# Seven half-size block products for the SwiGLU behind the convolution, and another spread of the adaLN chunks

## The chip, the cores and the metric

The kernel runs on one core of one Trainium2 chip, in one launch. The metric is the device time of an execution in microseconds (us). Of the kernel before there are three timed runs and one profiled execution. Engines are called as the profile calls them: PE (matrix products), PEld (its weight loads), DVE (VectorE), ACT (ScalarE), POOL (GpSimd), SP (SyncE, which issues nearly all transfers).

## The reference, cut to what matters

Two layers work on 256 latent tokens x and 256 context tokens z, 1024 features each. A layer is a SwiGLU, a token mixer (a short convolution in the first layer, attention in the second) and another SwiGLU, each between norms that shift, scale and gate by vectors made from a condition c (adaLN):

```python
mx = (silu(c) @ w_mod[i] + b_mod[i]).reshape(B, 9, 1, D)      # shift, scale, gate for three sublayers
mz = (silu(c_ctx) @ w_mod[i] + b_mod[i]).reshape(9, D)

def ffn_sublayer(x, mod, k, g_pre, g_post, w_gu, w_down):
    h = rmsnorm(x, g_pre) * (1 + mod[k + 1]) + mod[k]
    gu = h @ w_gu                                              # 1024 -> 2 * 2816
    y = (silu(gu[..., :2816]) * gu[..., 2816:]) @ w_down       # 2816 -> 1024
    return x + 0.5 * mod[k + 2] * rmsnorm(y, g_post)
```

All values are float32. The output is the latent stream.

## The kernel before

**Products.** Features lie on the 128 partitions, tokens along the free axis (512 columns: 256 of x, 256 of z). A float32 operand is split into a high part that the PE reads at full rate and the rest (`hi`, `lo`), and one product is three: hi·hi, lo·hi, hi·lo (lines 441 to 443, in `groups`). Weights come as slots: 512 KB, eight blocks of 128 by 128, loaded by SP, then split: ACT writes `whi` (line 252), DVE or POOL subtracts to get `wlo` (line 253). The set `POOL` names the slots whose subtraction POOL does. Eight split slots are held in a ring.

**Stages.** Stage 0 is the first SwiGLU, then comes the convolution, stage 2 is the SwiGLU behind it, stage 3 the first SwiGLU of the second layer; then attention and a last SwiGLU on x alone. The 22 gate/up tiles (128 hidden features each) of a SwiGLU are cut into three chunks (`CHUNKS`): gate/up of a chunk, then its share of the down projection in eight jobs of one output tile each. In the first chunk a job's result is copied into `y` by ACT, in the second DVE adds it (line 589), and the third goes through the tail, where the norms of x and z run beside products. Products go to four PSUM banks in turn (`ps`, four buffers): one bank per job of the down projection, two per gate/up tile.

**Head.** The first tiles of a stage are done for x alone while the norm of z still runs, then for z alone: 256-column products.

**Pairs.** In stage 3 alone (`SEVEN = {3: 4}`), tiles 4 to 21 go in nine pairs through `pair` (line 525 is its product): two tiles by 1024 features, times the two token halves, as a 2 by 2 block product in seven products of half size in place of eight (Strassen's way in Winograd's form). One product of the seven is 24 products of the PE at 256 columns. `forms` makes the four sums of the activations once, on DVE and ACT. A pair loads four raw slots; DVE adds weights (line 289, `summed`) and splits the sums (line 278), POOL subtracts for three raw slots (line 281, not by the set `POOL`), and DVE and ACT combine the results (lines 552 to 569). From the first stage with pairs on, raw slots alternate between two rings of three (`two_rings`).

**adaLN chunks.** The vectors come in 18 modules (`MODS`) of eight chunks. `mod_step` fetches the next 512 KB chunk (`wmd`, two buffers) and takes the product sum of the one before on DVE (`dot`, line 340): two sums per chunk in modules 0 to 13 (x and z), one in 14 to 17. `pacer` spreads the steps of a stage evenly over its jobs: `NMODS` says up to which module a stage goes. The jobs are the gate/up tiles outside head and pairs, and the 16 jobs of the first two down projections; `mods_until` does what is left before the tail. With `(7, 6, 15)` stage 0 takes 56 steps (its first 16 chunks come ahead), the convolution none, stage 2 takes 48 and stage 3 the last 24.

**Order.** PE's order is the order of the program text. On the other engines a scheduler orders the instructions; the product sums, the adds into `y` and the products with the gate (line 481) stay in program order among themselves.

Of the kernel before, what the change touches and what calls it, by code (L numbers as in the profile page):

```python
# [27 lines left out]
KT = D // P  # L28
# [1 line left out]
N = 2 * S  # L30
DFF = 2816
FT = DFF // P
CHUNKS = {0: ((0, 7), (7, 14), (14, 22)), 2: ((0, 7), (7, 14), (14, 22)), 3: ((0, 6), (6, 14), (14, 22))}

SEVEN = {3: 4}
HQ, HKV, HD = 16, 4, 64
GRID_W = 64
EPS = 1e-6
# [11 lines left out]
CONV_HEAD = 2  # L50
AT_TAIL = [(2.34, 3.97, 15.14, 16.36), (2.26, 3.97, 15.49, 17.43), (2.59, 3.6, 14.42, 17.25), (2.03, 2.96, 12.85, 16.35)]
AT_HEAD = [(2.1, 4.38, 12.64, 12.75), (3.64, 4.86, 13.86, 15.27), (3.45, 5.01, 14.82, 16.43), (1.54, 2.67, 12.39, 14.05)]
NMODS = (7, 6, 15)
PACE = 1
QUERIES = [(0, 1), (2, 3), (4,), (5,)]
LATE = 16
# [3 lines left out]
ATT = "s0 q6 s0 q7 x0 p s1 p s1 t00 x1 s2 r0 t01 t02 r1 s2 t03 v00 s3 v01 t10 t11 v02 s3 t12 v03 t13 v10 v11 t20 v12 s4 t21 v20 s4 v13 t22 t23 s5 t30 v21 s5 t31 v22 v30 v23 t32 t33 s6 t40 v31 s6 t41 v40 v32 o000 o001 t42 v41 v33 t43 o002 s7 t50 t51 o003 v50 v42 v43 s7 t52 t60 o010 v51 t53 t61 v52 v60 o011 t62 v53 t70 v61 t71 v62 t72 v70 t63 o012 v71 v63 t73 o013 v72 v73 o100 o101 o102 o103"  # L60
EXPT = 1
SCALE = "VAAG"
POOL = {0, 256, 2, 3, 1, 259, 260, 263, 264, 147, 148, 155, 156, 163, 165, 169, 170, 54, 56, 58, 60, 61, 64, 68, 71, 72, 78, 91, 92, 94, 95, 223, 97, 99, 230, 103, 104, 233, 106, 235, 108, 236, 240, 114, 243, 245, 246, 247, 248, 249, 255}

X = slice(0, S)
Z = slice(S, N)
# [15 lines left out]
def tiles_of(w):  # L82

    k, m = w.shape
    return w.reshape(k // P, P, m // P, P).transpose(2, 0, 1, 3)
# [14 lines left out]
def ffn_slots(w_gu, w_down, chunks, seven=FT):  # L100
    gu = tiles_of(w_gu)
    dn = tiles_of(w_down)
    out = []
    for a, b in chunks:
        c = min(max(a, seven), b)
        if a < c:
            out.append(slots_of(np.stack([gu[a:c], gu[FT + a:FT + c]], 1).reshape(-1, P, P)))
        for m in range(c, b, 2):

            for f, k in ((FT, 0), (0, 0), (0, 4), (FT, 4)):  # L110
                out.append(slots_of(gu[f + m:f + m + 2, k:k + 4].reshape(-1, P, P)))
        out.append(slots_of(dn[:, a:b].reshape(-1, P, P)))
    return out


def lay_out(i):
    f = np.float32
    w = []
    w += ffn_slots(i["ffn_w_gu"][0, 0], i["ffn_w_down"][0, 0], CHUNKS[0])

    w[0][:4] = slots_of(w[0][:4].reshape(4, P, KT, P).transpose(2, 0, 1, 3).reshape(-1, P, P))
    ci = tiles_of(i["conv_w_in"][0]).reshape(3, 8, KT, P, P)
    w.append(slots_of(ci[[1, 2, 0]].transpose(1, 0, 2, 3, 4).reshape(-1, P, P)))
    w.append(slots_of(tiles_of(i["conv_w_out"][0]).reshape(-1, P, P)))
    w += ffn_slots(i["ffn_w_gu"][0, 1], i["ffn_w_down"][0, 1], CHUNKS[2])
    w += ffn_slots(i["ffn_w_gu"][1, 0], i["ffn_w_down"][1, 0], CHUNKS[3], SEVEN[3])
    qkv = i["attn_w_qkv"][0]
    pm = q_perm()
    q = slots_of(tiles_of(qkv[:, pm]).reshape(-1, P, P))
    v = qkv[:, D + 256:].reshape(2, 4, P, 256).transpose(0, 2, 1, 3).reshape(2, P, 1024)  # L130
    w += [q[:6], slots_of(tiles_of(qkv[:, D:D + 256]).reshape(-1, P, P)), v, q[6:]]
    w.append(halves_of(i["attn_w_o"][0][pm]))

    gu = tiles_of(i["ffn_w_gu"][1, 1]).reshape(2, FT, KT, P, P)
    w.append(slots_of(gu.transpose(1, 0, 2, 3, 4).reshape(-1, P, P)))
    w.append(halves_of(i["ffn_w_down"][1, 1]))
    wst = np.concatenate(w, 0)

    wm = i["w_mod"].reshape(2, D, 9, D).transpose(0, 2, 3, 1)
    wm = np.stack([wm[l, c] for l, c, _ in MODS]).reshape(len(MODS), KT, P, D)  # L140


    front = wm[:2].copy()
    wm[0] = front[:, DOTS].transpose(1, 0, 2, 3).reshape(KT, P, D)
    wide = front[:, PAIRS].reshape(2, 2, 2, P, KT, P).transpose(1, 4, 5, 0, 2, 3).reshape(2, 4, 2, P, 512)
    wm[1] = wide.transpose(0, 1, 3, 2, 4).reshape(KT, P, D)
    bm = i["b_mod"].reshape(2, 9, KT, P)
    bm = np.stack([bm[l, c] for l, c, _ in MODS]).transpose(2, 0, 1)
    ng = i["norm_g"].reshape(12, KT, P).transpose(2, 0, 1)
    cw = i["conv_w"][0].reshape(3, KT, P).transpose(2, 0, 1)  # L150
    xz = np.concatenate([i["x"][0], i["ctx"][0]], 0).reshape(N, KT, P).transpose(2, 1, 0)


    d = np.arange(HD)
    axis, half, quar = d // 32, (d // 16) % 2, d % 16
    tok = np.arange(S)
    inv = f(10000.0) ** (-(np.arange(16, dtype=f)) / f(16))
    pos = np.stack([(tok // GRID_W).astype(f), (tok % GRID_W).astype(f)])
    ang = pos[axis] * inv[quar][:, None]
    cos = np.tile(np.cos(ang), (2, 1)).astype(f)  # L160
    sin = np.tile(np.sin(ang), (2, 1)).astype(f)
    rot = np.zeros((P, P), f)
    for o in range(P):
        if half[o % HD] == 0:
            rot[o + 16, o] = -1.0
        else:
            rot[o - 16, o] = 1.0
    a = np.arange(P)
    m0 = np.where(a[None, :] <= a[:, None], 0.0, -1e30).astype(f)
    m1 = np.where(a[:, None] <= a[None, :], 0.0, -1e30).astype(f)  # L170
    cst = np.concatenate([cos, sin, cos * f(HD ** -0.5), sin * f(HD ** -0.5), rot, m0, m1], 1)
    cc = np.stack([i["c"].reshape(D), i["c_ctx"].reshape(D)])
    cp = cc.reshape(2, KT, P).transpose(2, 1, 0)
    vec = np.concatenate([cp.reshape(P, -1), bm.reshape(P, -1), ng.reshape(P, -1), cw.reshape(P, -1)], 1)
    arrays = dict(xz=xz, wst=wst, wmd=wm.reshape(-1, P, D), vec=vec, cst=cst, cc=cc.reshape(1, 2 * D),
                  snk=i["attn_sink"].reshape(1, HQ))
    return {k: np.ascontiguousarray(a) for k, a in arrays.items()}
# [6 lines left out]
class Kernel:  # L184
# [427 lines left out]
        return self.norms(1, y, parts[1], nxt)  # L612

    def pacer(self, nmods, njobs):
        todo = nmods * KT - self.mod_at
        state = [0, 0]

        def pace(weight=1):
            state[0] += weight
            while state[1] < min(todo, -(-todo * state[0] // njobs)):  # L620
                self.mod_step()
                state[1] += 1
        return pace

    def ffn(self, l, j, nxt, nmods, pending):
# [4 lines left out]
        m0 = sum(map(len, HEADS[3 * l + j - 1][0])) if pending else 2  # L630
        pace = self.pacer(nmods, PACE * (SEVEN.get(3 * l + j, FT) - m0) + 16)
        if 3 * l + j == min(SEVEN):
            self.two_rings = base
        forms = None
        for ci, (a, b) in enumerate(CHUNKS[3 * l + j]):
            nk = b - a
# [9 lines left out]
            else:  # L646
                for _ in self.gate_up(ALL, base, range(m0), act):
                    next(start, None)
            seven = SEVEN.get(3 * l + j, FT) - a
            for m in range(m0, min(nk, seven)):  # L650
                self.weave([self.gate_up(ALL, base, [m], act)])
                pace(PACE)
            if 3 * l + j in SEVEN and forms is None:
                forms = self.forms()
# [586 lines left out]
```

## Time and profile before

| | us |
|---|---|
| median of three runs | 1683.94 |
| lowest, highest | 1678.51, 1684.57 |
| profiled execution | 1679.4 |
| its span | 1677.6 |
| PE busy | 1631.8 (97%) |
| DVE busy | 1142.7 (68%) |
| ACT busy | 695.4 (41%) |
| POOL busy | 321.6 (19%) |

The profiled execution is a fourth run of its own; its span is what its instructions cover. On PE the page counts products as overlapping, so one product is shown longer than it takes in a row; the time of a stretch divided by the products in it tells what one costs.

### The profile page before, as it was taken

The numbers are of one execution on the slowest core, as the hardware profiler recorded it, in microseconds if no ns is written. First come the engines' busy times: TensorE is split into PE (matmuls) and PEld (weight loads), VectorE is DVE, ScalarE is ACT, GpSimd is POOL, SyncE is SP. The second block draws the span as 40 slices with busy tenths as digits, with TensorE's granted clock in tenths as the row PEclk, the third lists the DMA queues.
The fourth block names the chain that finished last, engine by engine and source line by source line (L and its number), as shares of the span: only waits on it lengthen the run. The fifth ranks groups of instructions, "written<-read, shape, count | busy, mean of one in ns | idle before, by whom it ended". The sixth has DMA issues, their size and how long they took to land.

```text
span 1677.6 us, 25175 instructions
## 1 busy us (share of the span) xinstructions
PE 1631.8 (97%) x10026; PEld 1439.4 (86%) x10026; DVE 1142.7 (68%) x1747; ACT 695.4 (41%) x1166; POOL 321.6 (19%) x214
## 2 busy tenths in 40 slices
PE   8899999999999999999999998999999989989998
PEld 3688888889988998888888998899899887889987
DVE  7769779866744365876965489387785678665553
ACT  4522221325423643322222444354255558654442
POOL 1100000125102431000110421231232664130000
PEclk9999999999999999999999999999999999999999
DMA  9556556653232215664664215334634221045550
GB/s 354 170 169 225 191 186 215 200 175 102 88 101 89 76 52 175 214 193 157 213 199 158 84 50 191 124 101 155 210 103 137 93 88 64 26 164 193 193 181 25
DMA packets 70313, 246.83 MB, mean 147 GB/s; under 512 B 7730, under 2 KB 10290, under 8 KB 70196
## 3 DMA queue, kind: packets, MB, share of 16 engines
q1 hardware_dynamic: 69908, 245.02, 43.8%
q8 instruction: 78, 1.28, 0.3%
q14 instruction: 39, 0.32, 0.1%
q10 hardware_dynamic: 288, 0.20, 0.0%
HBM read 244.15 MB, written 1.05 MB: 146 GB/s over the span
## 4 chain that ended last, share of the span: by engine, by line
PE 88%; DVE 6%; ACT 2%; issue 1%; POOL 1%; DMA 1%; SPq 0%; DVEq 0%; POOLq 0%; ACTq 0%
PE mm L443 23%; PE mm L442 23%; PE mm L441 23%; PE mm L525 10%; DVE junk L340 1%; PE po L947 1%; PE mm L1071 1%; PE mm L1072 1%; PE mm L1070 1%; PE tp L933 1%; POOL acc L402 1%; PE mm L893 1%; DMA xr<-in_xz 1%; DVE wlo L253 1%; PE prb L361 0%
## 5 line engine op out<-in xcount | busy, mean ns | idle before, releaser
L441 PE MATMUL mm<-hh,whi 128*128 128x512 f32 (+1 forms) x1232 | 436.8, 355 | 6.2 <-ACT hh L451 5.0
L252 ACT ACTIVATE whi<-raw 128x1024 fp32r<-128x1024 f32 x280 | 292.3, 1056 | 355.7 <-PE mm L443 291.5
L443 PE MATMUL mm<-hl,whi 128*128 128x512 f32 (+1 forms) x1232 | 435.0, 353 | 1.6 <-DVE hl L416 1.5
L442 PE MATMUL mm<-hh,wlo 128*128 128x512 f32 (+1 forms) x1232 | 435.1, 353 | 0.0
L253 DVE TENSOR_TENSOR wlo<-raw,whi 128x1024 fp32r<-128x1024 f32 x229 | 290.7, 1279 | 113.8 <-ACT whi L252 112.5
L340 DVE CUSTOM_DVE_ANT_0 junk<-wmd,sc,vec 128x1024 bf16<-128x1024 f32 x232 | 307.9, 1327 | 20.4 <-DMA wmd<-in_wmd 16.7
L443 PE MATMUL mm<-al,whi 128*128 128x256 f32 (+1 forms) x848 | 275.9, 325 | 3.3 <-DVE al L569 3.3
L441 PE MATMUL mm<-ah,whi 128*128 128x256 f32 (+1 forms) x848 | 277.0, 327 | 1.7 <-ACT ah L568 1.7
L442 PE MATMUL mm<-ah,wlo 128*128 128x256 f32 (+1 forms) x848 | 275.8, 325 | 0.0
L253 POOL TENSOR_TENSOR wlo<-raw,whi 128x1024 fp32r<-128x1024 f32 x51 | 128.2, 2518 | 753.6 <-ACT whi L252 750.0
L441 PEld LDWEIGHTS mm<-hh,whi 128*128 128x128 f32 x1232 | 233.4, 189 | 42.4 <-ACT hh L451 6.3
L443 PEld LDWEIGHTS mm<-hl,whi 128*128 128x128 f32 x1232 | 233.5, 190 | 34.1 <-DVE hl L416 2.1
L442 PEld LDWEIGHTS mm<-hh,wlo 128*128 128x128 f32 x1232 | 233.7, 190 | 32.7
L443 PEld LDWEIGHTS mm<-al,whi 128*128 128x128 f32 x848 | 161.0, 190 | 18.4 <-DVE al L569 4.8
L441 PEld LDWEIGHTS mm<-ah,whi 128*128 128x128 f32 x848 | 161.1, 190 | 16.5 <-ACT ah L568 2.1
L442 PEld LDWEIGHTS mm<-ah,wlo 128*128 128x128 f32 x848 | 161.1, 190 | 13.6
L479 ACT ACTIVATE sg<-mm 128x512 f32<-128x512 f32 (+1 forms) x78 | 38.6, 495 | 227.4 <-PE mm L443 227.3
L481 DVE TENSOR_TENSOR pr<-mm,sg 128x512 f32<-128x512 f32 (+1 forms) x78 | 43.7, 560 | 128.7 <-PE mm L443 81.5
L281 POOL TENSOR_TENSOR wlo<-raw,whi 128x1024 fp32r<-128x1024 f32 x27 | 68.3, 2530 | 215.7 <-ACT whi L280 199.8
L443 PE MATMUL mm<-h,whi 128*128 128x256 f32 x352 | 99.0, 281 | 0.0
L441 PE MATMUL mm<-h,whi 128*128 128x256 f32 x352 | 98.9, 281 | 0.0
L442 PE MATMUL mm<-h,wlo 128*128 128x256 f32 x352 | 98.7, 280 | 0.0
(226 smaller groups left out, 2480.0 us busy)
## 6 DMA issues: line engine op xcount, KB each, us to landing
raw<-in_wst SPq DMA_DIRECT2D x316, 512.0 KB, 3.6
wmd<-in_wmd SPq DMA_DIRECT2D x140, 512.0 KB, 4.1
xr<-in_xz SPq DMA_DIRECT2D x2, 1024.0 KB, 9.9
wmq<-in_wmd SPq DMA_DIRECT2D x8, 256.0 KB, 7.8
out_y<-xt SPq DMA_DIRECT2D x3, 256.0 KB, 2.1
rtab<-in_cst SPq DMA_DIRECT2D x1, 512.0 KB
out_y<-xt SPq DMA_DIRECT2D x2, 128.0 KB, 1.9
msk<-in_cst ACTq DMA_DIRECT2D x1, 192.0 KB, 4.1
```

What stands on the lines that cost most here:

```text
L252: nc.scalar.activation(hi, raw, AF.Copy)
L253: d = sub.tensor_tensor(lo, raw, hi.bitcast(F32), ALU.subtract)
L281: self.nc.gpsimd.tensor_tensor(lo, src, hi.bitcast(F32), ALU.subtract)
L340: self.keep(self.nc.vector.tensor_tensor_reduce(junk, wt, self.sc[v], 1.0, b, ALU.mult, ALU.add, out))
L402: nc.gpsimd.tensor_tensor(acc, acc, sq, ALU.add)
L441: nc.tensor.matmul(pt[:, :n], whi, rhi[:, sl], start=i == 0, stop=False)
L442: nc.tensor.matmul(pt[:, :n], wlo, rhi[:, sl], start=False, stop=False)
L443: nc.tensor.matmul(pt[:, :n], whi, rlo[:, sl], start=False, stop=i == last)
L479: nc.scalar.activation(sg[:, :n], pg[:, :n], AF.Silu)
L481: self.keep(nc.vector.tensor_mul(pr[:, :n], pu[:, :n], sg[:, :n]))
L525: mm = lambda w, r, start=False, stop=False: nc.tensor.matmul(out, w, r, start=start, stop=stop, skip_group_check=True)
L893: nc.tensor.matmul(sp[e], act[4 * p2 + 2 * jp + jj][x][rows[e], qs], kt[p2][w][rows[e], :], start=a == 0, stop=False)
```

## The change

Stage 2 gets what stage 3 has: `SEVEN` names it too, its chunks become 6, 8 and 8 tiles, and its weights are laid out for `pair`. The raw slots take two rings from stage 2 on. `NMODS` becomes `(8, 11.25, 13.5)`: with module counts in fractions (hence the `int`), stage 0 takes 64 steps, the convolution 10, stage 2 takes 18 and stage 3 takes 36. In stage 3 four of these have two sums each, the other 32 one: 40 sums where there were 24. In stage 2 the 18 steps have 36 sums where there were 88. From the set `POOL` six slots of stage 2 go: 106, 108, 147, 148 and 155 are raw slots of pairs now, 114 is one of the first down projection.

```diff
-CHUNKS = {0: ((0, 7), (7, 14), (14, 22)), 2: ((0, 7), (7, 14), (14, 22)), 3: ((0, 6), (6, 14), (14, 22))}
-
-SEVEN = {3: 4}
+CHUNKS = {0: ((0, 7), (7, 14), (14, 22)), 2: ((0, 6), (6, 14), (14, 22)), 3: ((0, 6), (6, 14), (14, 22))}
+
+SEVEN = {2: 4, 3: 4}
...
-NMODS = (7, 6, 15)
+NMODS = (8, 11.25, 13.5)
...
@@ lay_out
-    w += ffn_slots(i["ffn_w_gu"][0, 1], i["ffn_w_down"][0, 1], CHUNKS[2])
+    w += ffn_slots(i["ffn_w_gu"][0, 1], i["ffn_w_down"][0, 1], CHUNKS[2], SEVEN[2])
...
@@ pacer
-        todo = nmods * KT - self.mod_at
+        todo = int(nmods * KT) - self.mod_at
```

DVE in stage 2, where the first chunk's gate/up ends and its down projection begins. Before, `pr` and `al` finish tile 6 there, between a subtraction for a coming slot and two sums of an adaLN chunk (`junk`, two per chunk):

```order
L481 TENSOR_TENSOR pr<-mm,sg 128x512
L253 TENSOR_TENSOR wlo<-raw,whi 128x1024
L452 TENSOR_TENSOR al_5043<-pr,ah_5042 128x512
L340 ISA junk,mod_1_0_5686<-wmd,sc_95,vec 128x1024
L340 ISA mod_1_0_5686 128x1
L340 ISA junk,mod_1_1_5687<-wmd,sc_96,vec 128x1024
```

Now the first chunk's only pair ends there, and these rows run from the combining of its products to the first two of its four `al` (line 569):

```order
L563 TENSOR_TENSOR mm<-gz,mm 128x512
L560 TENSOR_TENSOR mm<-mm,gx 128x512
L340 ISA junk,mod_2_1_4521<-wmd,sc_96,vec 128x1024
L340 ISA mod_2_1_4521 128x1
L253 TENSOR_TENSOR wlo<-raw,whi 128x1024
L289 TENSOR_TENSOR sum<-raw 128x512 x2
L569 TENSOR_TENSOR al_5155<-mm,ah_5154 128x256 x2
L340 ISA junk,mod_2_0_4520<-wmd,sc_95,vec 128x1024
L340 ISA mod_2_0_4520 128x1
L569 TENSOR_TENSOR al_5157<-mm,ah_5156 128x256 x2
```

The four `al`, which the down projection reads, stand behind the combining, the sums of weights (`sum`) and, counted from the stage's head on, nine sums of adaLN chunks. In stage 3 eight such sums stood ahead of the last `al`, now nine.

DVE in stage 0, second down projection, from the first add into `y` to the second:

```order
L589 TENSOR_TENSOR y<-y,mm 128x512
L340 ISA junk,mod_5_0_1501<-wmd,sc_95,vec 128x1024
L340 ISA mod_5_0_1501 128x1
L340 ISA junk,mod_5_1_1502<-wmd,sc_96,vec 128x1024
L340 ISA mod_5_1_1502 128x1
L334 SCALAR_TENSOR_TENSOR mod_5_0_1501<-mod_5_0_1501,vec 128x8
L589 TENSOR_TENSOR y<-y,mm 128x512
```

The same stretch of the changed kernel:

```order
L589 TENSOR_TENSOR y<-y,mm 128x512
L340 ISA junk,mod_7_0_1689<-wmd,sc_95,vec 128x1024
L340 ISA mod_7_0_1689 128x1
L340 ISA junk,mod_7_1_1690<-wmd,sc_96,vec 128x1024
L340 ISA mod_7_1_1690 128x1
L253 TENSOR_TENSOR wlo<-raw,whi 128x1024
L340 ISA junk,mod_7_0_1689<-wmd,sc_95,vec 128x1024
L340 ISA mod_7_0_1689 128x1
L340 ISA junk,mod_7_1_1690<-wmd,sc_96,vec 128x1024
L340 ISA mod_7_1_1690 128x1
L589 TENSOR_TENSOR y<-y,mm 128x512
```

Between these two adds stand four sums in place of two, and a subtraction. Over the eight adds, from the first to the last, 20 sums and 7 subtractions became 24 and 8.

DVE in stage 3, second down projection, at the same place:

```order
L589 TENSOR_TENSOR y<-y,mm 128x512
L340 ISA junk,mod_6_0_9309<-wmd,sc_95,vec 128x1024
L340 ISA mod_6_0_9309 128x1
L253 TENSOR_TENSOR wlo<-raw,whi 128x1024
L340 ISA junk,mod_6_0_9309<-wmd,sc_95,vec 128x1024
L340 ISA mod_6_0_9309 128x1
L589 TENSOR_TENSOR y<-y,mm 128x512
```

The same stretch of the changed kernel:

```order
L589 TENSOR_TENSOR y<-y,mm 128x512
L340 ISA junk,mod_7_0_10326<-wmd,sc_95,vec 128x1024
L340 ISA mod_7_0_10326 128x1
L253 TENSOR_TENSOR wlo<-raw,whi 128x1024
L340 ISA junk,mod_7_0_10326<-wmd,sc_95,vec 128x1024
L340 ISA mod_7_0_10326 128x1
L340 ISA junk,mod_7_0_10326<-wmd,sc_95,vec 128x1024
L340 ISA mod_7_0_10326 128x1
L589 TENSOR_TENSOR y<-y,mm 128x512
```

Here three sums, each of another chunk, stand where two stood; over the whole down projection and just behind it 18 chunks in place of 12.

## Rows read from the trace of the kernel before

**Rows 1.** The page: span, busy time by engine, and shares of the last chain.
```profile
span 1677.6 us, 25175 instructions
PE 1631.8 (97%) x10026; PEld 1439.4 (86%) x10026; DVE 1142.7 (68%) x1747; ACT 695.4 (41%) x1166; POOL 321.6 (19%) x214
...
PE 88%; DVE 6%; ACT 2%; issue 1%; POOL 1%; DMA 1%; SPq 0%; DVEq 0%; POOLq 0%; ACTq 0%
```

**Rows 2.** Stretches: the length behind the window, then busy time by engine.
```profile
core 0: us, PE busy (x) PEld busy (x) DVE busy (x) ACT busy (x) POOL busy (x), PEclk, DMA share, GB/s
447.90:546.80 98.90, 98.90 (x435) 81.16 (x434) 45.05 (x52) 30.77 (x39) 12.14 (x5) 1.00 0.32 107
611.50:914.50 303.00, 303.00 (x1443) 253.71 (x1442) 214.52 (x298) 89.76 (x120) 18.40 (x7) 1.00 0.55 178
...
826.60:914.50 87.90, 87.90 (x386) 72.13 (x385) 56.47 (x72) 24.72 (x31) 11.17 (x4) 1.00 0.58 187
985.40:1281.50 296.10, 288.62 (x2078) 272.03 (x2077) 223.79 (x342) 139.73 (x230) 70.72 (x28) 0.98 0.42 141
985.40:1017.40 32.00, 29.51 (x231) 28.69 (x230) 30.64 (x53) 14.32 (x29) 2.49 (x1) 0.95 0.06 21
...
1037.30:1077.70 40.40, 35.42 (x146) 27.84 (x145) 19.15 (x32) 12.11 (x20) 4.83 (x2) 0.92 0.49 165
1157.50:1201.70 44.20, 44.20 (x194) 36.03 (x194) 33.34 (x49) 9.80 (x14) 6.23 (x2) 1.00 0.60 203
1201.70:1281.50 79.80, 79.80 (x673) 79.78 (x672) 64.14 (x96) 47.22 (x77) 27.24 (x11) 1.00 0.44 146
238.60:277.00 38.40, 38.40 (x169) 31.51 (x168) 36.37 (x54) 7.95 (x8) 0.00 (x0) 1.00 0.68 219
```

**Rows 3.** Waits of PE in stage 3's head for z: total, times, longest.
```profile
PE mm L443 <- DVE hl L416: 1.5, 2, 1.0
PE mm L441 <- ACT hh L415: 1.0, 1, 1.0
```

**Rows 4.** Timeline of PE behind stage 3's first pair: start, duration, instruction, [idle <-releaser].
```profile
1042.31 0.40 PE L442 MATMUL mm<-ah,wlo 128*128 128x512 f32 x1
1045.76 0.79 PE L443 MATMUL mm<-al,whi 128*128 128x512 f32 x1 [3.05 <-DVE al L569]
...
1047.63 0.79 PE L443 MATMUL mm<-al,whi 128*128 128x512 f32 x1 [0.22 <-DVE al L569]
1048.22 0.63 PE L441 MATMUL mm<-ah,whi 128*128 128x512 f32 x1
```

**Rows 5.** DVE from 1017.4 to 1047.6 by groups: count, busy, mean ns, idle before.
```profile
L340 DVE CUSTOM_DVE_ANT_0 junk<-wmd,sc,vec 128x1024 bf16<-128x1024 f32 x8 | 11.7, 1467 | 0.6 <-DMA wmd<-in_wmd 0.6
L253 DVE TENSOR_TENSOR wlo<-raw,whi 128x1024 fp32r<-128x1024 f32 x5 | 6.1, 1218 | 0.1
```

**Rows 6.** Timelines of DVE and of POOL from 1022 to 1026.
```profile
1023.12 2.81 DVE L340 CUSTOM_DVE_ANT_0 junk<-wmd,sc,vec 128x1024 bf16<-128x1024 f32 x1
...
1022.09 2.76 POOL L281 TENSOR_TENSOR wlo<-raw,whi 128x1024 fp32r<-128x1024 f32 x1 [0.98 <-ACT whi L280]
```

**Rows 7.** Lines 340 and 310 from 985 to 1210: ns or us min/median/max.
```profile
L340 DVE CUSTOM_DVE_ANT_0 junk<-wmd,sc,vec x24: 1270/1280/3301, 1021.3 to 1205.3; 128x1024 bf16<-128x1024 f32 x24
...
  DMA wmd<-in_wmd: 7.0, 6
...
DMA to landing us min/median/max: 3.4/4.4/5.9
```

**Rows 8.** Timeline of DVE in stage 3's second down projection.
```profile
1164.78 0.68 DVE L589 TENSOR_TENSOR y<-y,mm 128x512 f32<-128x512 f32 x1
1165.38 1.28 DVE L340 CUSTOM_DVE_ANT_0 junk<-wmd,sc,vec 128x1024 bf16<-128x1024 f32 x1
1166.59 0.08 DVE L340 DVE_READ_ACCUMULATOR2_ANT mod<- 128x1 f32 x1
```

**Rows 9.** Line 589 from 240 to 296: ns, first and last start.
```profile
L589 DVE TENSOR_TENSOR y<-y,mm x8: 680/684/685, 247.8 to 289.2; 128x512 f32<-128x512 f32 x8
```

**Rows 10.** Line 281: POOL's subtractions in the pairs.
```profile
L281 POOL TENSOR_TENSOR wlo<-raw,whi x27: 2402/2416/3269, 1008.3 to 1265.7; 128x1024 fp32r<-128x1024 f32 x27
```

More of the change, by code (lines that the diff above doesn't have):

```diff
@@ L62 @@
 SCALE = "VAAG"
-POOL = {0, 256, 2, 3, 1, 259, 260, 263, 264, 147, 148, 155, 156, 163, 165, 169, 170, 54, 56, 58, 60, 61, 64, 68, 71, 72, 78, 91, 92, 94, 95, 223, 97, 99, 230, 103, 104, 233, 106, 235, 108, 236, 240, 114, 243, 245, 246, 247, 248, 249, 255}
+POOL = {0, 256, 2, 3, 1, 259, 260, 263, 264, 156, 163, 165, 169, 170, 54, 56, 58, 60, 61, 64, 68, 71, 72, 78, 91, 92, 94, 95, 223, 97, 99, 230, 103, 104, 233, 235, 236, 240, 243, 245, 246, 247, 248, 249, 255}
 X = slice(0, S)
```

## Prediction

> **What bounds the kernel now.** I read the page's busy shares first. PE is busy for 1631.8 of 1677.6 us, and it holds 88% of the chain that ended last; DVE has 6%, all others together 6% [rows 1]. So the time is the number of products by their spacing, plus the few places where PE starves. Next I cut the span into stretches, to see what a product costs and where PE falls behind. In stage 2, from the head for z to the end of the last gate/up tile, PE is busy in all of the 303.0 us. The same work in stage 3, with nine pairs, takes 296.1, of which PE is busy in 288.6 only [rows 2]. That difference, 6.9, is the like-for-like worth of the change to stage 2, if stage 2 meets the same hindrances.
>
> How large it could be follows from the spacing. The last eight tiles of stage 2 take 87.9, so one takes 10.99 and two take 21.98; four pairs in stage 3 take 79.8, so one takes 19.95 [rows 2]. A pair saves 2.03 us, nine save 18.2. About 11.3 of that is lost in stage 3, and two windows hold it. In the head for z 231 half-size products at 0.1188 (79.80/672) would be 27.4 us; it takes 32.0. There `hl` and `hh` are late behind the forms [rows 3], DVE is busy for 30.6 of the 32.0, and the granted clock is 0.95. That is 4.6. In the first down projection 144 products at 0.2285 (87.90/384, rounded) would be 32.9; it takes 40.4, at a clock of 0.92 [rows 2]. That is 7.5: PE stands for 3.05 us until DVE delivers an `al` of the first pair, and more in front of it (from 1042.3 to 1048.2 it runs only a few products), and then products come slower for a while [rows 4]. 4.6 and 7.5 are 12.1, which is the 11.3 within 0.8.
>
> What makes that `al` late? In the 30 us before it DVE does eight adaLN sums (11.7 us) and five subtractions (6.1), with 0.6 of waiting for a chunk [rows 5]. One of those sums takes 2.81 us in place of 1.28, while an operation of POOL runs beside it [rows 6].
>
> **The change, part by part.**
>
> *Stage 2.* Stage 2 gets the chunks 6, 8, 8, the four tiles of head, the nine pairs and so the 2078 products of stage 3. I take the 303.0 to become 296.1: **-6.9**. Two things differ from stage 3 as it is. The order has nine sums ahead of the last `al`, where stage 3 had eight: one more at 1.28 + 0.08 [rows 8]. The nine come from five chunks, two sums each, so fewer transfers are waited for: the 0.6 goes. Net +0.8, and since DVE was busy throughout, all of it on the path: **-6.1** for the stage. Bounds: if nothing of the two losses returned, -18.2; if a pair's first stall doubled (4.8 of waits more), -1.3. I take the like-for-like value, which is a row of this very code.
>
> POOL's added work is 27 subtractions at 2.416, 65 us [rows 10], in a stretch where it was busy for 18.4 of 303 [rows 2]; hidden, with the five or six subtractions that DVE and the pairs take over from it. If that cover went, each late `wlo` would hold PE up by at most the 2.4 it lasts.
>
> Rows 6 are worth weighing with a page. The sum of 1.28 took 2.81, and began 1 us after POOL's subtraction and ended with it. The Trainium skill says in "SBUF — State Buffer", section "Who interferes with whom", that DVE and GpSimd share one port pair, taken for a whole instruction, so that a DVE operation with two SBUF inputs and a GpSimd operation that reads SBUF shut each other out. This trace agrees in that place; by that rule each of the 27 new subtractions could hold one sum, which is the third rival below.
>
> *Stage 3.* Its first chunk has nine sums ahead of the last `al` in place of eight, from as many chunks: +1.36 less the 0.6 of waiting that falls elsewhere, **+0.8**. Behind that `al`, now at 1048.4 (1047.6 [rows 4] + 0.8), come 13 chunks. Two buffers, a landing of 4.4 (median) and 1.36 for the sum give a chunk each (4.4 + 1.36)/2 = 2.88 us [rows 7, 8]; the 13 are done at 1085.8. The first operation of DVE that PE needs then is for the fifth product of the next pair, 1078.5 + 4 x 2.85 = 1089.9 (2.85 is 19.95/7). Cost 0; with the longest landing, 5.9 [rows 7], a chunk takes 3.63 and it would be 5.7 late.
>
> In the second down projection 18 chunks, one sum each, stand where 12 did. At 2.88 they want 51.8 us where the stretch has 44.2 [rows 2], so they run past it: two have landed at 1165.4 [rows 8], 16 follow at 2.88, then two sums and an add, 1214.8. Three more operations of 0.68 (one of them the length of an add [rows 9]) stand before the bank that the seventh product of the next pair needs, at 1201.7 + 6 x 2.85 = 1218.8. So 1.9 us are left at the median landing; at 5.9 it is 10.1 late. I take **+1.0**, near the median's end, since half the landings are longer. The end point is a landing of 4.4 + 2 x 1.9/16 = 4.6, very near the median: this term is the shakiest.
>
> The Trainium skill gives in "DMA: Bandwidth & Descriptors", section "Anatomy of one DMA — SWDGE (gpsimd) path", a fit of 2.0 us plus the bytes by 436e3 per us. For 512 KB that is 3.2, an estimate, and a chunk would take 2.28, so that 18 (41 us) fit into 44.2 with no lag. The trace has 4.4 at the median with weights loading beside it, and differs; the measurement decides, and the sum above goes by it.
>
> *Stage 0.* In the second down projection DVE is busy for 36.4 of 38.4 us [rows 2]. Its eight adds into `y` start from 247.8 to 289.2 [rows 9]: the last comes 12 us after PE has finished. Between them now stand four sums and a subtraction more: 4 x 1.36 + 1.22 [rows 8, 5] = 6.7, so the last add starts at 295.9 and ends at 296.5. There are four banks; of the next two gate/up tiles, the second's second product needs the bank of that add, at 277.0 + 10.99 + 5.49 = 293.5. It is 3.0 late: **+3.0**. Bounds: 0, if the 2.0 of idle time and operations of DVE that can wait make room, and 6.7, if an add before the last one is already late.
>
> *Convolution.* Ten steps with two sums each, 20 x 1.36 = 27 us, go into a stretch of 98.9 us in which DVE is busy for 45.1, PE throughout [rows 2]. Hidden: 0; it would be 27 only if each stood in PE's way. *Stage 2's second down projection* has 20 sums, as many as stage 0's before, and there nothing stalled: 0. The chunks are the same in number; only their place moves.
>
> **Sum.** -6.1 + 0.8 + 1.0 + 3.0 = **-1.3** us. From the profiled execution, 1679.4 (span 1677.6 and 1.8 around it), it makes 1678.1. That execution lies 4.5 under the median of the three timed runs, 1683.94; against the median the same sum gives **1682.6**, which I predict. No change is what lies within 0.5%, 8.4 us, about what a measurement of this kernel can tell.
>
> **Rivals.**
>
> 1. *The first pair's stall does not return in stage 2.* PE's wait there is 3.05 and less in front of it [rows 4]; a few operations of DVE decide it. For it: stage 2's first sums come from five chunks already there, with half the transfers, and the 2.81 of rows 6 is a matter of phase. Against it: the operations ahead of `al` are otherwise those of stage 3, and DVE has no gaps. Without the 7.5 it makes -8.8 and 1675.1; if the head's 4.6 went too (the norms' forms wait on nothing but DVE and ACT), -13.4 and 1670.5.
> 2. *Chunk transfers set the pace of stage 3: slower.* 36 steps of one sum each need 36 transfers in 16 jobs. If landings there move to the longest seen, 5.9, the second down projection is 10.1 late and the first 5.7: -6.1 + 0.8 + 3.0 + 10.1 + 5.7 = +13.5, 1697.4. It decides above a landing of 4.6 in the second. For it: the stretch already has DVE waiting for chunks (7.0 us of waits, six of them, [rows 7]) and moves 203 GB/s, the most of stage 3's rows here [rows 2]. Against it: before the change landings of 4.4 kept up, and weights load less when PE is held up.
> 3. *POOL's new subtractions hold DVE's sums* in the first chunks: 1.53 more (2.81 - 1.28) for one more sum in each of two stages, +3.1, so +1.8 and 1685.7. Against it: stage 3 already has such a collision inside its 296.1.
>
> **How the numbers follow.** My sum has 0.55. Its own range: stage 3's second down projection from 0 to some 6, stage 0's from 0 to 6.7, the stage-2 loss less or more by about 4; 1676 to 1691. Rival 1 has 0.28, since the difference is between a stall of a few microseconds and none. Rival 2 has 0.11, rival 3 0.06. Faster by over 0.5% (below 1675.5) is rival 1, 0.28; slower by over 0.5% (above 1692.4) is rival 2, 0.11; between lie 0.61. The range for 8 in 10 leaves out the half of rival 1 that also spares the head, and most of rival 2: 1671 to 1693.
>
> **What would show it.** In the changed profile stage 2's stretch from its head for z should take 297 us, its head 32 and its first down projection about 41, with PE waiting for `al` and a clock below 1. Near 289 there, rival 1 is right. In stage 0 PE should wait for an add (line 589) near 293, by about 3; none means that term is 0. In stage 3, a wait of PE for the combining near 1215 (shifted), with landings of `wmd` above 4.6 in the same stretch, is rival 2. The convolution's 98.9 should stay. The prediction is wrong altogether if PE waits in the convolution, or if a pair in stage 2 costs more than 19.95.

## The result and the profile after

The changed kernel takes 1690.54 us (median of five runs, 1688.70 to 1694.66); beside it the kernel before took 1679.97. The ratio is 1.0067 with a 95% interval of 1.0051 to 1.0083: slower, where 1682.6 and no change were predicted. The profiled execution takes 1689.8, its span is 1688.0, 10.4 more than before. The page, answering to [rows 1]:

```profile
span 1688.0 us, 26848 instructions
PE 1622.5 (96%) x10674; PEld 1461.3 (87%) x10674; DVE 1234.8 (73%) x1925; ACT 746.0 (44%) x1281; POOL 375.5 (22%) x235
...
PE 80%; DVE 11%; issue 3%; ACT 2%; DMA 2%; POOL 1%; SPq 0%; DVEq 0%; ACTq 0%; POOLq 0%
```

PE is busy for 9.3 us less, and yet the span is longer: the products were saved, and PE stands still for longer. On the chain DVE has 11% where it had 6%, and DMA 2%. To see where, here are stretches as in [rows 2] (length, busy times, granted clock, share of DMA, GB/s). First come the eight tiles behind stage 0's second down projection, the convolution's head for z and the rest of the convolution; then stage 2: whole, its head for z, its first down projection; then stage 3: the same three and its last eight tiles:

```profile
276.60:365.40 88.80, 88.11 (x385) 72.00 (x384) 80.25 (x109) 24.95 (x31) 16.76 (x6) 1.00 0.67 213
...
430.80:459.30 28.50, 22.72 (x164) 21.10 (x162) 27.68 (x53) 8.73 (x18) 0.00 (x0) 0.94 0.47 146
459.30:558.30 99.00, 99.00 (x434) 81.24 (x434) 52.72 (x67) 31.41 (x40) 12.73 (x5) 1.00 0.41 134
...
623.90:919.70 295.80, 288.84 (x2091) 272.00 (x2090) 240.56 (x369) 139.60 (x232) 71.70 (x28) 0.99 0.40 130
623.90:654.80 30.90, 29.23 (x244) 28.62 (x243) 28.90 (x54) 14.85 (x31) 3.08 (x1) 1.00 0.08 23
674.70:715.90 41.20, 35.91 (x146) 27.87 (x145) 26.70 (x41) 12.41 (x20) 4.94 (x2) 0.92 0.45 152
...
990.80:1291.50 300.70, 289.54 (x2080) 272.71 (x2079) 246.09 (x375) 138.90 (x230) 69.82 (x28) 0.98 0.49 160
990.80:1021.30 30.50, 28.01 (x231) 27.19 (x230) 28.40 (x53) 14.28 (x29) 3.08 (x1) 1.00 0.08 21
1041.30:1082.90 41.60, 36.18 (x146) 28.36 (x145) 32.53 (x48) 12.05 (x20) 4.82 (x2) 0.92 0.69 238
1206.70:1291.50 84.80, 81.55 (x674) 81.33 (x673) 71.07 (x105) 47.02 (x77) 26.86 (x11) 0.98 0.49 161
```

Stage 2 does what was forecast: 303.0 becomes 295.8, -7.2. Stage 3 goes from 296.1 to 300.7, +4.6, and its last eight tiles alone give +5.0 (79.8 before, 84.8 now); its other parts nearly cancel. The largest item is where nothing was expected: the convolution's head for z takes 28.5, +9.8. Before it was this row:

```profile
429.20:447.90 18.70, 18.70 (x164) 18.59 (x163) 14.01 (x30) 9.25 (x19) 0.00 (x0) 1.00 0.24 83
```

With +0.9 in the eight tiles behind stage 0's second down projection (87.9 before) and +1.1 in stage 0's tail and the head for x behind them (64.3 before, 65.4 now) these make 9.2 of the 10.4; the rest is spread over stretches that are alike in both.

PE stands still for 5.8 of the 28.5 us, and its 164 products are busy for 22.7 in place of 18.7, at a mean granted clock of 0.94. What PE waited for there, in total, times and longest (before there was no wait):

```profile
PE mm L443 <- DVE hl L416: 3.9, 4, 1.4
PE mm L441 <- ACT hh L415: 1.9, 3, 0.7
```

DVE's timeline there (start, duration, instruction):

```profile
431.87 1.28 DVE L340 CUSTOM_DVE_ANT_0 junk<-wmd,sc,vec 128x1024 bf16<-128x1024 f32 x1
...
433.07 0.87 DVE L416 SCALAR_TENSOR_TENSOR hl<-ut,mod,hh 128x256 fp32r<-128x256 f32 x2
433.86 0.42 DVE L745 TENSOR_TENSOR cu<-mm,sg 128x256 f32<-128x256 f32 x1
434.19 1.28 DVE L340 CUSTOM_DVE_ANT_0 junk<-wmd,sc,vec 128x1024 bf16<-128x1024 f32 x1
...
435.39 0.88 DVE L414 SCALAR_TENSOR_TENSOR ut<-xr,mod,prb 128x256 f32<-128x256 f32 x2
```

And the group of line 340 in the head's stretch (shortest, median and longest in ns, first and last start):

```profile
L340 DVE CUSTOM_DVE_ANT_0 junk<-wmd,sc,vec x12: 1277/1282/1287, 431.9 to 457.2; 128x1024 bf16<-128x1024 f32 x12
```

Twelve of the convolution's 20 sums start in the head: seven between the first `ut` of the norm of z (431.08) and its last `hl` (446.80), five behind that among the operations of the head's tiles. One more starts just ahead, at 428.71. POOL's `rr`, a small operation of the same norm, began beside it and took 1.72 us in place of 0.70, and PE waited 0.9 for it; that is most of the +1.1 ahead of the head. In the program these sums come behind the head, in jobs of the full tiles; the scheduler put them there, since the first chunks had landed (DVE waits for no chunk in the head) and nothing keeps a sum behind the norm.

Behind stage 3's second down projection one wait stands out, of PE for `gx`, 3.2 us. The chain through that place, in order of time:

```profile
1207.51 1.28 DVE junk L340
...
1208.84 3.48 DMA wmd<-in_wmd
...
1212.45 2.29 DVE junk L340
...
1218.37 1.27 DVE junk L340
...
1219.65 0.62 DVE sum L289
...
1220.30 0.03 ACT whi L277
...
1220.79 0.60 ACT gx L548
...
1221.43 8.66 PE mm L525 x58
```

Read it from the end: the fifth product of a pair goes into a bank that ACT's `gx` has to read first; `gx` stands in ACT's queue behind `whi` of a sum of weights; that sum (line 289) stands on DVE behind adaLN sums; and the first of those wait for chunks, each fetched when the sum before has given back its buffer. The landings there, answering to [rows 7]:

```profile
L310 SPq DMA_DIRECT2D wmd<-in_wmd x17: 327/328/328, 1171.7 to 1217.2; - x17
...
DMA to landing us min/median/max: 3.3/3.5/4.6
```

### The profile page after: what moved, and what is told of

It reads as the page before. It is cut to its first block, busy times and chain, and to the rows that moved or that the text cites. A ratio compares the mean times of both kernels' runs of the same rounds, so it can differ in the third digit from the quotient of the medians.

```text
span 1688.0 us, 26848 instructions
## 1 busy us (share of the span) xinstructions
PE 1622.5 (96%) x10674; PEld 1461.3 (87%) x10674; DVE 1234.8 (73%) x1925; ACT 746.0 (44%) x1281; POOL 375.5 (22%) x235
## 3 DMA queue, kind: packets, MB, share of 16 engines
q8 instruction: 83, 1.36, 0.3%
## 4 chain that ended last, share of the span: by engine, by line
PE 80%; DVE 11%; issue 3%; ACT 2%; DMA 2%; POOL 1%; SPq 0%; DVEq 0%; ACTq 0%; POOLq 0%
PE mm L525 18%; PE mm L443 18%; PE mm L441 18%; PE mm L442 17%; DVE junk L340 3%; DMA wmd<-in_wmd 2%; PE po L947 1%; PE mm L1071 1%; PE mm L1072 1%; PE mm L1070 1%; DVE wlo L253 1%; PE tp L933 1%; DVE sum L289 1%; POOL acc L402 1%; PE mm L893 1%
## 5 line engine op out<-in xcount | busy, mean ns | idle before, releaser
L340 DVE CUSTOM_DVE_ANT_0 junk<-wmd,sc,vec 128x1024 bf16<-128x1024 f32 x232 | 323.2, 1393 | 31.6 <-DMA wmd<-in_wmd 28.6
L441 PE MATMUL mm<-hh,whi 128*128 128x512 f32 (+1 forms) x944 | 325.9, 345 | 9.2 <-ACT hh L451 5.0
L443 PE MATMUL mm<-hl,whi 128*128 128x512 f32 (+1 forms) x944 | 322.0, 341 | 7.1 <-DVE hl L416 6.7
L442 PE MATMUL mm<-hh,wlo 128*128 128x512 f32 (+1 forms) x944 | 322.3, 341 | 0.0
L443 PEld LDWEIGHTS mm<-hl,whi 128*128 128x128 f32 x944 | 179.0, 190 | 30.6 <-DVE hl L416 8.6
L442 PEld LDWEIGHTS mm<-hh,wlo 128*128 128x128 f32 x944 | 179.4, 190 | 19.7
L525 PE MATMUL mm<-hh,whi 128*128 128x256 f32 x576 | 161.9, 281 | 3.2 <-ACT gx L548 3.2
L525 PE MATMUL mm<-tf,whi 128*128 128x256 f32 x864 | 161.8, 284 | 0.0
L525 PE MATMUL mm<-hl,whi 128*128 128x256 f32 x576 | 161.3, 280 | 0.0
L525 PE MATMUL mm<-hh,wlo 128*128 128x256 f32 x576 | 161.2, 280 | 0.0
L525 PEld LDWEIGHTS mm<-tf,whi 128*128 128x128 f32 x864 | 137.4, 192 | 0.0
```

Source lines behind the costliest of these rows:

```text
L340: self.keep(self.nc.vector.tensor_tensor_reduce(junk, wt, self.sc[v], 1.0, b, ALU.mult, ALU.add, out))
L441: nc.tensor.matmul(pt[:, :n], whi, rhi[:, sl], start=i == 0, stop=False)
L442: nc.tensor.matmul(pt[:, :n], wlo, rhi[:, sl], start=False, stop=False)
L443: nc.tensor.matmul(pt[:, :n], whi, rlo[:, sl], start=False, stop=i == last)
L525: mm = lambda w, r, start=False, stop=False: nc.tensor.matmul(out, w, r, start=start, stop=stop, skip_group_check=True)
```

## The experiments

All are edits of the changed kernel unless said otherwise. `keep` is the helper with which the kernel keeps operations of an engine in program order among themselves. Three groups: the items that made it slower, the first pair, and a version made from what was found. I compare stretches first: spans of single profiles scatter by some us where nothing was edited. Stage 0's first down projection starts between 118.7 and 123.2 us in kernels that have the same spread in stage 0, at 118.7 and 120.1 in two profiles of one kernel (the version with both orders).

**The convolution's head.** The last `hl` of its norm of z joins the chain of kept operations, to which the sums belong (`d` is that `hl`, line 416):

```diff
+            if nxt == (0, 1) and v == 1 and k == KT - 1:
+                self.keep(d)
```

> The changed kernel, but on DVE the sums of the convolution's adaLN chunks stay behind the last hl of the norm of z (that hl joins the chain of operations that keep the program's order). Theory A, the sums stood in the way of hl and ut: the convolution's head for z goes from 28.5 back to about 18.7 us with no wait for hl, and the time falls by about 10, to 1681. Theory B, it is the transfers: the chunks' fetches hold back SP's loads of weights from 415 to 452, and PE would wait for those in place of hl; the head stays above 25 and the time above 1687.

Measured: 1683.50 (ratio to the kernel before 1.0016, 0.9993 to 1.0039); the span is 1681.6. The head:

```profile
431.20:450.50 19.30, 19.30 (x164) 19.18 (x163) 17.80 (x36) 8.80 (x17) 0.00 (x0) 1.00 0.26 87
```

9.2 us of the 9.8 are back and PE waits for nothing there. Four sums now stand in the head, all behind the last `hl`; the other 16 are among the full tiles, which still take 99.0. `rr` takes 0.70 again. Theory A holds for the head. The whole falls by 7, not 10; in the profile, stage 3's head for z took 32.6 at a granted clock of 0.90, 30.5 at 1.00 in the one above, and the rest lies in other stretches that the edit does not touch.

**The spread by itself.** The kernel before, with the new spread (and the `int` that it needs) alone:

```diff
-NMODS = (7, 6, 15)
+NMODS = (8, 11.25, 13.5)
```

> The kernel before with the new spread of the adaLN steps alone (64, 10, 18, 36), pairs in stage 3 only. Theory A, the loss of the changed kernel is the spread's: +9.8 in the convolution's head for z, +4.6 in stage 3, +1 in stage 0, and stage 2 as before, 303: +15, about 1695. Theory B, as the forecast had it, the spread costs 1 in stage 3's second down projection, 0.8 at its first pair and 3 in stage 0, and nothing in the convolution: about 1685.

Measured: 1701.51, ratio 1.0118 (1.0083 to 1.0153), span 1695.9; theory A had about 1695. Three of its stretches, the convolution's head, stage 2 and stage 3's last eight tiles:

```profile
430.70:458.40 27.70, 22.60 (x165) 20.78 (x163) 27.39 (x53) 8.79 (x18) 0.00 (x0) 0.94 0.45 148
622.90:925.90 303.00, 303.00 (x1443) 253.73 (x1442) 147.26 (x192) 89.58 (x120) 16.85 (x7) 1.00 0.40 128
1215.10:1300.80 85.70, 81.62 (x674) 81.42 (x673) 69.81 (x107) 47.00 (x77) 28.09 (x11) 0.98 0.48 161
```

The losses of the changed kernel in these two places are the spread's: +9.0 and +5.9 here, without any pair in stage 2. And the pairs are worth 7.2 us in stage 2 (303.0 against 295.8); the spans differ by 1695.9 - 1688.0 = 7.9.

**The pairs by themselves**, with the old spread:

```diff
-NMODS = (8, 11.25, 13.5)
+NMODS = (7, 6, 15)
```

> The changed kernel with the old spread (56, 0, 48, 24): the pairs of stage 2 alone. The convolution's head is 18.7 again and stage 3 takes 296. Theory A, DVE's whole work decides: stage 2 has 88 sums in place of 36, 25 more in each of its two down projections (34 us of DVE, where the changed kernel's second has 40.9 of 44.2 and its first some 27 of 41), so each runs 20 to 30 us past its end into the pairs, whose own DVE work is 64 of 80; the pairs behind each lose 10 to 20. 1690 to 1705. Theory B, sums fit beside the pairs: stage 2 takes 296 and the time is 1673.

Measured: 1724.49, ratio 1.0252 (1.0216 to 1.0287). Stage 2's eight tiles, second down projection and last eight tiles:

```profile
704.70:801.40 96.70, 83.55 (x673) 82.57 (x672) 87.93 (x131) 44.30 (x75) 25.17 (x10) 0.93 0.45 153
801.40:857.40 56.00, 46.16 (x194) 37.06 (x194) 50.74 (x78) 10.91 (x16) 6.53 (x2) 0.94 0.53 169
857.40:959.20 101.80, 85.74 (x672) 84.91 (x673) 88.43 (x130) 45.75 (x75) 27.27 (x11) 0.92 0.51 171
```

In the changed kernel they take 79.8, 44.2 and 79.8. Theory A in kind, but larger than I gave it (10 to 20 in the pairs behind each down projection, at most 1705): PE loses 17, 12 and 22 us. The adds into `y` and the combining of a pair are late as well: in these stretches PE waits 14.5 us for adds into `y` and 14.5 for `al` of pairs. So most of the 88 sums had to leave stage 2; the question is where to.

**Stage 3's load.**

```diff
-NMODS = (8, 11.25, 13.5)
+NMODS = (8, 11.25, 15)
```

> The changed kernel with 30 adaLN steps in stage 2 and 24 in stage 3 (18 and 36 in the changed kernel). Theory A, a second down projection costs time as soon as DVE's whole work in it overflows: stage 3's wait of 3.5 behind it goes (-4.9, and -1 at the first pair), but stage 2's second down projection has 30 sums in place of 16, 40.9 + 14 x 1.36 = 60 us of DVE work in 44.2, and loses about 5 in the same place: about 1690. Theory B, the pace of transfers alone decides (18 chunks at one sum each overflowed, 15 at two sums each take 15 x 3.1 = 46 and do not): 1685.

Measured: 1687.73, ratio 1.0046 (1.0026 to 1.0066). The stretches are stage 2's first down projection and last eight tiles, and the same of stage 3:

```profile
673.50:715.70 42.20, 37.08 (x147) 28.80 (x147) 38.77 (x60) 12.43 (x20) 5.87 (x2) 0.88 0.60 199
839.60:923.60 84.00, 80.53 (x674) 79.91 (x673) 72.28 (x108) 46.57 (x77) 26.74 (x11) 1.00 0.50 165
1046.10:1086.10 40.00, 35.27 (x147) 27.70 (x146) 18.85 (x31) 11.99 (x19) 4.82 (x2) 0.96 0.48 167
1210.00:1289.90 79.90, 79.90 (x674) 79.88 (x673) 64.23 (x96) 47.24 (x77) 27.49 (x11) 1.00 0.45 145
```

Stage 3 is at 79.9 again, and stage 2's last eight tiles lose 4.2. Both theories rested on a miscount, though: half of the chunks in that second down projection have one sum, so that 24 sums from 16 fetches stand in and behind it, where the changed kernel has 20 from 10, not 30 from 15. Sums and fetches grew together, and the time lies between the two forecasts: this run shows that the loss moves with the steps, and does not tell sums from transfers. The next two do.

**Transfers or sums, in stage 3.** Two kernels halve one of the two and leave the other. The first takes the sum of every second one-sum chunk over the chunk before once more, without a fetch; the second sums every second one over 64 of its 1024 columns. Each leaves out part of the computation, and each ran once (1681.22 and 1685.51 us).

```diff
+        if m >= 14 and j % 2:
+            wt = self.mod_last
```

> The changed kernel, but in modules 14 to 17 (the one-sum chunks of stage 3) every second chunk is not fetched; its sum is taken over the chunk before again, so the sums stay 36 and their transfers are halved (these vectors are left out of the computation). Theory A, the transfers of one-sum chunks pace DVE: the wait of 3.5 in the pairs behind stage 3's second down projection goes and the eight tiles take 79.8 in place of 84.8. Theory B, the number of sums that stand ahead of the sums of weights on DVE decides: 84 or more, as before.

```diff
-            self.dot(..., self.mods[l, c][v][:, j:j + 1])
+            self.dot(..., self.mods[l, c][v][:, j:j + 1], 64 if m >= 14 and j % 2 else D)
```

> The counterpart: all chunks of modules 14 to 17 are fetched, but every second one is summed over 64 of its 1024 columns only (the rest of these sums is left out), so that 1.1 us of DVE go per two chunks. Theory A, transfers pace DVE: a little over half of the 4.9 us stays (chunks at 4.4/2 + 0.7 in place of 2.98 us). Theory B, DVE's work decides: 79.8 for the eight tiles, no wait.

Measured, the last eight tiles and DVE's wait for chunks in and behind the second down projection, with half the fetches, and then with half the sums (the changed kernel: 84.8, and 9.8 in 10 waits):

```profile
1204.70:1284.60 79.90, 79.90 (x674) 79.86 (x673) 66.50 (x98) 47.10 (x77) 26.95 (x11) 1.00 0.42 139
...
DVE junk L344 <- DMA wmd<-in_wmd: 0.9, 1, 0.9
```

```profile
1207.20:1287.70 80.50, 80.14 (x674) 79.90 (x673) 67.85 (x103) 46.54 (x77) 26.58 (x11) 1.00 0.50 163
...
DVE junk L340 <- DMA wmd<-in_wmd: 17.8, 13, 2.9
```

With half the fetches the loss is gone though all the sums stay, even three that POOL's subtractions stretch to 3.31, 2.45 and 2.52 us; so the transfers were part of it, as theory A says, and theory B alone falls. With half the sums it goes too, to 0.6, where A wanted some 2.5 to stay, although DVE then waits longer for chunks. Neither is the bound by itself. My reading is that a buffer is held through its landing, its wait in DVE's queue and its sum, and that with two buffers the chunks finish in time if either part shrinks. A third buffer, the direct test, was not tried.

**The first pair.** Its four `al` are kept, so that they stay ahead of the sums that come behind them in the program:

```diff
-                nc.vector.tensor_tensor(lo[:, h], t[:, c], hi[:, h].bitcast(F32), ALU.subtract)
+                d = nc.vector.tensor_tensor(lo[:, h], t[:, c], hi[:, h].bitcast(F32), ALU.subtract)
+                if len(act) == 2 and self.first_pair:
+                    self.keep(d)
...
+                self.first_pair = ci == 0
```

> The changed kernel, but in the first chunk of stages 2 and 3 the pair's four al keep their place ahead of the adaLN sums of the down projection behind them; nine sums, 12 us of DVE, move from in front of the last al to behind it. Theory A, these sums make al late: the first down projections of stages 2 and 3 fall from 41.2 and 41.6 to about 33, 8 us each; in stage 3 the 18 chunks then all come behind al, at 2.98 us each 54 us, and run some 10 us past the start of the next pair, which costs up to that much there. 1675 to 1684. Theory B, DVE is late by its other work (forms, sums of weights, subtractions): the waits for al stay, and the time stays within 3 of 1690.

Measured: 1685.14, ratio 1.0015 (0.9995 to 1.0035). The two first down projections, and stage 3's two groups of eight tiles:

```profile
671.40:708.40 37.00, 35.11 (x147) 28.05 (x146) 32.71 (x50) 12.26 (x20) 4.82 (x2) 0.95 0.54 171
1034.50:1069.60 35.10, 33.67 (x146) 26.80 (x145) 30.12 (x44) 12.22 (x20) 4.87 (x2) 1.00 0.60 195
1069.60:1154.10 84.50, 82.05 (x673) 81.49 (x672) 69.53 (x106) 44.21 (x75) 24.76 (x10) 0.98 0.51 162
1198.30:1285.10 86.80, 82.42 (x673) 82.22 (x672) 69.34 (x107) 47.25 (x77) 27.75 (x11) 0.96 0.50 160
```

-4.2 and -6.5, and then +4.7 and +2.0: the sums did hold `al`, and in stage 3, with 36 chunks, what was saved came back in the pairs behind. The time lies between the two theories' ranges; of the span's -6.6, 2.4 lie ahead of stage 0's first down projection, where nothing was edited. The same edit on the kernel before, whose stage 3 has 24 steps:

> The kernel before with one change: the four al of stage 3's first pair keep their place ahead of the adaLN sums behind them. Its stage 3 has 24 steps, so no transfers run past a down projection. Theory A, the stall at the first pair was those sums: the first down projection falls from 40.4 to about 35, and nothing comes back later: -5, about 1675. Theory B, the sums only move their cost to the next pairs: no change, within 2. What this leaves between it and the kernel with both orders and the new spread, 1661, is what the pairs of stage 2 are worth once nothing stalls: by A 14.

Measured: 1677.34, ratio 0.9982 (0.9961 to 1.0004). The first down projection takes 34.9 (40.4 before) and the pairs behind it 79.7 and 79.8, so in the trace all of it stays saved, as A has it; in the time the interval reaches to no change. This profiled execution cannot be compared by its span: from 123 to 369 us its products came 2% slower (246.0 for what took 242.0), at a granted clock of 1.00 as before; why stays open.

**A version from these.** Both orders, and a spread that fills the convolution, which had room, and spares stage 3:

```diff
-NMODS = (8, 11.25, 13.5)
+NMODS = (8, 12, 15)
```

> The pairs in stage 2 with both changes of order (the sums behind the norm of z in the convolution, and behind the first pair's al in stages 2 and 3), and a spread of 64, 16, 24 and 24 steps. By the measured parts: from a span of 1681.6 with the norm first, -4.8 and -6.5 at the two first down projections, -5 behind stage 3's second, up to +3 for 12 sums more in stage 2, nothing for 12 more in the convolution (DVE has about 45 of 99 us free there): a time of 1665 to 1670. The rival: the sums only move their cost to the next pairs, as they did in stage 3 with al first, and the time is not under 1676.

Measured: 1661.21, ratio 0.9880 (0.9836 to 0.9923), span 1658.7. The convolution's head, its full tiles, the two first down projections, and stage 3's last eight tiles:

```profile
426.70:446.00 19.30, 19.30 (x164) 19.17 (x162) 17.81 (x37) 8.87 (x18) 0.00 (x0) 1.00 0.27 85
446.00:545.00 99.00, 99.00 (x434) 81.23 (x433) 78.23 (x112) 32.09 (x40) 12.64 (x5) 1.00 0.60 191
662.90:700.50 37.60, 35.66 (x147) 28.23 (x146) 33.34 (x48) 12.26 (x20) 4.79 (x2) 0.95 0.52 168
1027.80:1064.70 36.90, 35.38 (x147) 28.06 (x146) 25.68 (x40) 12.36 (x20) 4.81 (x2) 0.95 0.66 214
1188.60:1268.30 79.70, 79.70 (x673) 79.70 (x672) 64.13 (x96) 47.21 (x77) 27.38 (x11) 1.00 0.47 145
```

Of the 32 sums now in the convolution, 28 stand in the full tiles, where they fill DVE to 78 of 99 us and cost PE nothing, and four in the head behind the last `hl`. Without the pair's order:

> The version with both orders and the spread 64, 16, 24, 24, without al first at the pairs. Theory A, the parts add up: its two first down projections take 41 to 42 again in place of 37.5 and 36.8, so about 8 more than 1661: 1669. Theory B, with fewer sums in stage 3 the stall there is gone anyway: 1665 or less.

Measured: 1675.38, ratio 0.9979 (0.9964 to 0.9994), span 1669.4; the first down projections take 41.7 and 40.3. Theory A by the stretches: they lose 4.1 and 3.4, 7.5 in all, where about 8 was expected. The spans differ by 10.7, but the last SwiGLU, which the order does not touch, took 188.0 us in the profile above and 192.5 in this one. The time is 6 above theory A's 1669. A second measurement of the version with both orders:

> The version with both orders and the spread 64, 16, 24, 24 once more, beside the other: its first measurement was 1661 with a ratio of 0.984 to 0.992, more than its parts' sum from the profiles (a span of 1665 and 1.8). By the parts the ratio is 0.991 to 0.993; if 0.988 holds, the parts leave out some 5 us.

Measured: 1665.47, ratio 0.9920 (0.9889 to 0.9951), span 1660.3: the sum of the parts holds. The first measurement came out lower; in its profile the last SwiGLU took 188.0 us, here 192.7. Beside it, the last loss that the prediction had named, in the heads for z:

```diff
-            nc.vector.tensor_tensor(hf[:, k], hi, lo, ALU.add)
+            self.keep(self.nc.vector.tensor_tensor(self.hf[:, k], hi, lo, ALU.add))
```

These sums stand in the program ahead of the head for z now, and the last `hl` of the norm of z is kept in stages 2 and 3 too.

> The version with both orders and the spread 64, 16, 24, 24, and in the heads of stages 2 and 3 the whole norm of z stands ahead of the first sums hh + hl of the forms. Theory A, hl was late behind these sums: PE's waits for hl there (0.7 + 1.1 + 1.1 in stage 3, some 2.5 in stage 2) go, and the two heads come to 28.5 and 28 to 29, from 32.4 and 32.7: -4 to -7 in all, 1655. Theory B, the later forms hold up the first pair by as much: no change, within 2.

Measured: 1663.90, ratio 0.9908 (0.9882 to 0.9935), where theory A had 1655. The two heads, which took 32.4 and 30.5 in the version beside it:

```profile
611.50:640.40 28.90, 27.70 (x242) 27.50 (x241) 27.66 (x45) 12.59 (x27) 2.75 (x1) 1.00 0.07 19
972.40:999.50 27.10, 27.10 (x232) 27.06 (x230) 25.64 (x47) 12.17 (x25) 1.08 (x1) 1.00 0.07 21
```

-3.5 and -3.4; the head of stage 3 has no wait left. About half does not reach the span, which is 3.1 shorter: 1.6 come back at the two first pairs, whose sums come later; the first down projections take 35.9 and 37.3 in place of 37.8 and 35.3, together the same; stage 2's tail takes 1.1 more. The intervals of the two times overlap: the mechanism is shown, the gain is not.

## Why the prediction was wrong

Two steps of the prediction failed: the convolution, put at 0, which measured +9.8, and stage 3's second down projection, put at +1.0, which measured +4.8 (44.2 and the 79.8 behind it became 44.0 and 84.8). In both, sums that the new spread put there stand on DVE in front of operations that PE waits for.

The measured 1690.5 lies inside the range 1671 to 1693 all the same, and that is luck. The range was laid about the median of three runs, 1683.94; beside the changed kernel the kernel before had 1679.97. From there the same sum gives 1678.7 and the same range 1667 to 1689.

*Stage 2, -6.1*: right, and 1.1 short. 303.0 became 295.8; its head took 30.9, its first down projection 41.2, and PE waited 2.9 us for the `al` of the first pair, as stage 3 does. Rival 1, that this stall would not return, is refuted; its cause, the adaLN sums in front of `al`, is shown by the run with `al` first (37.0 and 35.1). That DVE is simply full of other work does not hold.

*Stage 3's first pair, +0.8*: 40.4 became 41.6, +1.2; the head ahead of it fell by 1.5, with the granted clock at 1.00 in place of 0.95.

*Convolution, 0*: this step failed, with +9.8 the largest error; PE's waits there are the sign by which the prediction called itself wrong altogether. "Hidden" was taken from the busy time of a stretch, 45 of 99 us, and from the place of the steps in the program. The stretch left out the head. The order on DVE says otherwise: 12 of the 20 sums start in the head, seven of them in front of operations of the norm on which its products wait. The price is near what those seven make: 7 x 1.36 = 9.5 us. The cover was real where the text had put the sums: in the run that keeps them behind the norm, 16 of them cost the full tiles nothing (99.0), and four behind the last `hl` leave the head at 19.3.

*Stage 3's second down projection, +1.0*: right in that a lag would arise there (rival 2's place), too small by 3.8. The pace was right: the sums came 2.80 us apart (18 intervals from 1170.42 to 1220.83), where 2.88 had been reckoned. But there are 19 of them in and behind the down projection (13 before), not 18 (12 before), and one more at 2.88 alone turns the 1.9 us left into 1.0 late. And the pace has another source than the one given: the landings were shorter, 3.5 in the middle, and three sums took 2.97, 2.20 and 2.29 beside POOL's subtractions. The Trainium skill, in "DMA: Bandwidth & Descriptors", section "Anatomy of one DMA — SWDGE (gpsimd) path", has a fit from which 3.2 follows for 512 KB, an estimate, for transfers that GpSimd issues. SP issues these; in the view above they have 3.3 to 4.6, and there was a lag all the same. What failed besides the count is the need: I had looked for the bank of the seventh product. What was late first were the sums of weights, which stand on DVE behind the adaLN sums and pass through ACT to the fifth product. "Decides above a landing of 4.6" was therefore no bound: the median landing is 3.5.

*Stage 0, +3.0*: +0.9. The down projection itself takes 38.4 as before; the loss is in the eight tiles behind it. The last add into `y` starts at 293.5 (289.2 before, 295.9 reckoned): DVE made room for a part. PE waits 0.7 at 282 for ACT (`sg`), not for the add.

*Conv and stage 2's covers on POOL, rival 3*: PE waited for no subtraction of POOL. In the first chunks of stages 2 and 3 one sum each ahead of the last `al` is stretched (2.82 and 2.81), as one was in stage 3 before, so rival 3 did not come where it was placed. But sums are stretched more often: the page has a mean of 1393 ns for the 232 sums of line 340, 1327 before, and the 2.29 stands in the chain above. Alone they do not make the loss, as the run with half the fetches shows; what share they have in it stays open. One reading of [rows 6] was off: the sum of 2.81 ended at 1025.93, 1.1 us behind POOL's subtraction (1024.85), not with it.

So the error is not in the pairs, which are worth what their row in stage 3 said, but in the sums that were moved to make room for them. Of the 11.7 us between the forecast and the span's change (10.4 and -1.3), 9.8 are the convolution's head and 3.8 stage 3's second down projection; -1.1, -2.1 and -1.1 are stage 2, stage 0 and stage 3's head with its first pair, +1.1 the stretch ahead of the convolution's head, which had no term; 1.3 is spread thin.

## What to carry to other kernels

Work that is moved into a stretch with idle time is hidden only where it stands: look up in the order of the engine whether it lands between operations of a chain that another engine waits for, and if it does, tie it behind the last of them. A busy share of a stretch prices the work, not its place. When a stage is made shorter on its main engine, ask first what was hidden under it, and where that goes; here the new place of the hidden work cost more than the shorter stage gave. With the norm's order alone set right the change is level with the kernel before (ratio 1.0016, 0.9993 to 1.0039); with another spread too it is 0.9979 (0.9964 to 0.9994), and with the pair's order as well 0.992 (0.989 to 0.995).

## What was not expected of the hardware

Stage 3's head for z, with the same waits of PE (2.3 to 2.5 us in three), took 30.5 us at a mean granted clock of 1.00 in the changed kernel and the one with `al` first, 32.0 at 0.95 in the kernel before, and 32.6 and 32.7 at 0.90 with the norm first and with both orders. No edit makes this: the two profiles of the version with both orders, one and the same kernel, have

```profile
975.20:1007.90 32.70, 30.37 (x232) 29.67 (x230) 30.77 (x53) 14.32 (x29) 2.49 (x1) 0.90 0.08 22
```

```profile
976.30:1006.80 30.50, 28.00 (x231) 27.19 (x230) 28.39 (x53) 14.29 (x29) 3.08 (x1) 1.00 0.08 21
```

In the first, behind the last of the three waits, some 25 products came 0.21 us apart, at 1.2 GHz; in the second they came 0.12 apart, at 2.4 GHz, behind the same waits. That is 2 us in one stretch of one profile. In the version whose head has no wait the clock was 1.00. And the granted clock does not tell all: in the last SwiGLU of these two profiles PE was busy for 181.5 us and for 186.2 with the same products, both at a granted clock of 0.99; why stays open.
